# The down projection of a convolutional feed-forward layer as seven products of halves

## The chip, the cores and the metric

The kernel runs on one core of a Trainium2 chip, in one launch. The metric is the device time of that launch in microseconds (us). The engines are named as in the profile: PE does matrix products (PEld are its weight loads), DVE is the vector engine, ACT the scalar engine, POOL is GpSimd, and SP issues most transfers.

## The reference, cut to what matters

Two transformer blocks run one after the other over 512 tokens of width 1024, in float32. The change touches the last layer of the first block:

```
FFN_DIM = 2816; FFN_CONV_K = 3
def conv_ffn(hn, w_up, conv_w, conv_b, w_down):
    u = causal_dwconv(hn @ w_up, conv_w) + conv_b     # (512, 5632)
    gate, val = jnp.split(u, 2, axis=-1)
    return (jax.nn.silu(gate) * val) @ w_down         # (512, 2816) @ (2816, 1024)
h = h + conv_ffn(rms_norm(h, norm_ffn), ffn_up, ffn_conv_w, ffn_conv_b, ffn_down)
```

The second block ends in a layer of the same kind without convolution: `square(relu(h @ w_ff1)) @ w_ff2`.

## The kernel before, in words

**Products.** Every float32 operand x is split into a high part h and a low part l (`wsplit` L163, `split` L177): ACT copies x into the rounded type (h), DVE subtracts h from x (l). A product of two tiles is then three matrix instructions, h·h, h·l and l·h (`mm3` L187). So one step of contraction of 128 over 512 columns costs three matmuls of 128x512.

**Up projection.** `gemm_f` (L196) takes one weight piece of 1024x128 at a time, splits it, and makes a tile of 128 channels x 512 tokens in one PSUM bank with 24 matmuls; then it hands the bank to an `evac` function. In `ffn_conv` (L502) that function is the convolution: ACT writes `u` from the bank (L511), DVE adds the two delayed taps (L513, twice). A gate tile then gets its SiLU on ACT; a value tile is multiplied by its gate tile (L530) and split into `ah`, `al`. Tiles come as two gates, then two values.

**Down projection.** The 22 channel tiles are worked in groups of 8, 8 and 6. After each group `gemm_w` (L252) adds that group's share to `h`: for each half of the output's columns it loads weight pieces of 256x512 and runs over four token tiles. 22 tiles x 2 halves x 4 token tiles x 3 are 528 matmuls. Each finished bank is added to `h` by DVE (`add_to` L1642), in the last group by the residual step `Residual.ev` (L417), which on ACT and POOL also gathers the sums for the next norm. `ev` calls `step` when a row tile is complete, and that starts the scaled copy of the row (`row`, L454) and its transposes (`turn`, L474) for the next stage.

**The seven products.** The last layer, `ffn_relu2` (L577), already has another form of the down projection, `gemm_s` (L279), with the helper `Halves` (L539). Tokens, contraction and columns are each cut in two, and seven products of halves take the place of eight. Their left operands are sums and differences of quarters of the activations (names A11, S3, A12, A22, S1, S2, S4; `Halves.put` builds them tile by tile: one subtraction for a tile of the first half of the contraction, three additions for one of the second half). Their right operands are quarters of the weights and differences of those (`less`, L301). A product runs into a pair of PSUM banks; some products run on top of an earlier one in the same pair, after that has been added to `h`. All second-half tiles are needed from the second product on, only A11 and S3 need none of them.

**What sets the order.** The instructions are written out by Python in program order; then a scheduler with its own cost model reorders them for each engine, and each engine runs its list strictly in turn. A buffer is reused when its last reader is done: split weights have three buffers in this stage (two of pool `w`, one of `w_ffn`), raw weights `wr` four, raw weights `ws` four.

Of the kernel before, what the change touches and what calls it, by code (L numbers as in the profile page):

```python
# [16 lines left out]
T = 512  # L17
# [54 lines left out]
class Lines:  # L72


    def __init__(self, p):
        self.p = p
# [12 lines left out]
class Core:  # L89
# [106 lines left out]
    def gemm_f(self, src, nk, n, xh, xl, evac, halves=None, pieces=(), wide=False):  # L196

        tok, pieces = xh.shape[2], list(pieces)
        step = 1024 // nk // 128 * 128
        tiles = []
        for c0 in range(0, n, step):
            wh, wl = pieces.pop(0) if pieces else self.wpiece(src[:, c0:min(c0 + step, n)], pool=wide and halves is not None)
            for c in range(0, wh.shape[2], 128):
                tiles.append(((c0 + c) // 128, wh[:, :, c:c + 128], wl[:, :, c:c + 128]))
            if halves is not None:
                if len(tiles) < 2:  # L210
                    continue
                pss = [self.gbank()[:, 0:tok] for _ in tiles]
                halves()
                halves = None
                for s in range(2):
                    ts = slice(s * tok // 2, (s + 1) * tok // 2)
                    for ps, (m, wh, wl) in zip(pss, tiles):
                        for k in range(nk):
                            self.mm3(ps[:wh.shape[2], ts], wh[:, k], wl[:, k], xh[:, k, ts], xl[:, k, ts], k == 0, k == nk - 1)
                for ps, (m, wh, wl) in zip(pss, tiles):  # L220
# [183 lines left out]
class Residual:  # L404
# [24 lines left out]
    def ev_s(self, t, c0, ps, last):  # L429
        if last:  # L430
            self.ev(t, c0, 512, ps)
        else:
            add_to(self.core, self.h)(t, c0, 512, ps)

    def step(self, t):

# [65 lines left out]
def ffn_conv(core, pool, h, xh, xl, up, conv_w, conv_b, down, mid, res):  # L502
# [4 lines left out]

    def conv(s, i, ps):
        w, o = taps[s]
        u = pool.tile([128, T], F32, name=f"u{s}", bufs=4)  # L510
        nc.scalar.activation(u, ps, AF.Identity, scale=w[:, o[2] + i:o[2] + i + 1], bias=w[:, o[3] + i:o[3] + i + 1])  # L511
        for d in (1, 2):
            nc.vector.scalar_tensor_tensor(u[:, d:], ps[:, 0:T - d], w[:, o[2 - d] + i:o[2 - d] + i + 1], u[:, d:], op0=ALU.mult, op1=ALU.add)  # L513
        return u

    for f0 in range(0, nf, 8):
        n = min(8, nf - f0)
        ah = pool.tile([128, 8, T], F32R, name="ah", bufs=2)
        al = pool.tile([128, 8, T], F32R, name="al", bufs=2)
        for p0 in range(f0, f0 + n, 2):  # L520
            gate = {}

            def ev_gate(m, ps):
                u = conv(0, p0 + m, ps)
                nc.scalar.activation(u, u, AF.Silu)
                gate[m] = u

            def ev_val(m, ps):
                u = conv(1, p0 + m, ps)
                nc.vector.tensor_tensor(u, u, gate[m], op=ALU.mult)  # L530
                core.split(ah[:, p0 + m - f0], al[:, p0 + m - f0], u)

            yield from core.gemm_f(up[:, p0 * 128:p0 * 128 + 256], 8, 256, xh, xl, ev_gate, mid if p0 == 0 else None, wide=True)
            yield from core.gemm_f(up[:, F + p0 * 128:F + p0 * 128 + 256], 8, 256, xh, xl, ev_val, wide=True)

        yield from core.gemm_w(down[f0 * 128:(f0 + n) * 128], n, D, ah[:, 0:n], al[:, 0:n], *((add_to(core, h),) if f0 + n < nf else (res.ev, 2)))


class Halves:  # L539


    def __init__(self, core, pool):
        self.core, self.pool = core, pool

    def open(self, n):

        self.n = n // 2
        a, b = ([self.pool.tile([128, m, 4, 256], F32R, name=f"a{x}{m}") for x in "hl"] for m in (2, 5))
        self.parts = a, b
        self.ops = {nm: [x[:, i, 0:self.n] for x in p] for p, nms in ((a, ("A11", "S3")), (b, ("A12", "A22", "S1", "S2", "S4")))  # L550
                    for i, nm in enumerate(nms)}
# [2 lines left out]
    def room(self, m):  # L554

        if m < self.n:
            self.raw[m] = self.pool.tile([128, 3, 256], F32, name="r3", bufs=4)
            return self.raw[m][:, 0::2]
        self.raw[m] = self.pool.tile([128, 5, 256], F32, name="r5", bufs=2)
        return self.raw[m][:, 0:2]  # L560
# [16 lines left out]
def ffn_relu2(core, pool, h, xh, xl, up, down, mid, res):  # L577
    nc = core.nc
    nf = down.shape[0] // 128
    a = Halves(core, pool)  # L580
    for f0 in range(0, nf, 8):
        a.open(8)

# [7 lines left out]
        yield from core.gemm_s(down[f0 * 128:(f0 + 8) * 128], a.ops, res.ev_s if f0 + 8 == nf else lambda t, c0, ps, last: add_to(core, h)(t, c0, 512, ps))  # L591

# [1052 lines left out]
    return ev  # L1645


BUCKETS = 32
SKEW = 639

# [126 lines left out]
def first_rest(core, I):  # L1777
# [30 lines left out]
                drain(cross_attention(core, p, xh, xl, I["ca_wq"], core.kv, I["ca_wo"], res))  # L1808
    core.n_at = core.ctx.enter_context(ExitStack())
    d_h = core.tc.dram_tile([T, D], F32, name="d_h")  # L1810
    core.res = Residual(core, core.n_at.enter_context(core.pool("n_at")), h, I["norm_final"], I["g_attn_2"], d_h)
    core.d_h = d_h.rearrange("(t p) d -> p t d", p=128)

    def mid():
# [118 lines left out]
```

## Time and profile before

| what | us |
|---|---|
| median of 3 runs | 1988.88 |
| lowest and highest run | 1988.84, 1993.32 |
| the profiled execution, whole | 1998.17 |
| its span, first to last instruction | 1996.4 |
| the layer that is changed, from its first matmul to the last of the down projection | about 837 to 1208 of the span |
| the layer that already uses seven products | about 1612 to 1988 of the span |

All times in the rows below are counted from the start of that span. A row of a group of instructions gives their count, their busy time, the mean of one, and the idle time of the engine just before them with what ended it. Matmuls overlap, so a matmul of "0.39 us" does not take that long in a row of matmuls: the distance between two starts does.

### The profile page before, as it was taken

To read this page: it belongs to the slowest core of one execution; us is meant where nothing else is said; L and a number is where in the kernel's file an instruction comes from. 1 tells how busy PE (TensorE), PEld (TensorE's weight loads), DVE (VectorE), ACT (ScalarE), POOL (GpSimd) and SP (SyncE) were. 2 spreads that over 40 slices of the span, in tenths; PEclk is the share of its full clock that TensorE was granted. 3 is DMA by queue.
4 is the path that set the end of the run, shared out by engine and by line. 5 is a ranking of instruction groups with operands and counts; after the bars stand their busy time and mean duration, and the time that the engine had idled before them with its cause. 6 is when DMAs were issued, how large, how long until landed. Compare 5 with 4: busy or idle time off the path is not lost.

```text
span 1996.4 us, 27818 instructions
## 1 busy us (share of the span) xinstructions
PE 1937.1 (97%) x10748; PEld 1625.0 (81%) x10748; DVE 1227.7 (61%) x1979; ACT 884.3 (44%) x1498; POOL 322.3 (16%) x367
## 2 busy tenths in 40 slices
PE   6999999999899999999999998999999999999998
PEld 5777888888778988888888887888888888888886
DVE  3457453318966645465464556666789756876867
ACT  4533223335634444343242346557766433443434
POOL 1333223343330100200000003002243111000000
PEclk9999999999999999999999998999999999999999
DMA  6223222342365641332333335543222533315231
GB/s 172 75 69 82 75 77 90 111 149 61 101 194 193 191 137 43 108 95 94 97 95 95 95 95 164 151 123 99 62 62 82 185 121 115 112 57 159 82 98 43
DMA packets 280728, 215.02 MB, mean 108 GB/s; under 512 B 28206, under 2 KB 239812, under 8 KB 280468
## 3 DMA queue, kind: packets, MB, share of 16 engines
q1 hardware_dynamic: 261364, 205.23, 34.0%
q10 hardware_dynamic: 19232, 8.02, 1.7%
q8 instruction: 85, 1.39, 0.3%
q14 instruction: 47, 0.39, 0.1%
HBM read 195.35 MB, written 20.48 MB: 108 GB/s over the span
## 4 chain that ended last, share of the span: by engine, by line
PE 88%; DVE 6%; ACT 3%; issue 2%; POOL 1%; SPq 0%; DMA 0%; ACTq 0%; DVEq 0%; POOLq 0%
PE g L190 49%; PE s L190 27%; PE s L725 1%; PE s L739 1%; PE s L378 1%; PE p L1008 1%; DVE sbr L809 1%; PE s L713 1%; PE s L712 1%; DVE ptl L181 1%; PE o L1138 0%; PE s L1144 0%; SPq L1718 0%; PE s L1393 0%; DVE sba L810 0%
## 5 line engine op out<-in xcount | busy, mean ns | idle before, releaser
L173 ACT ACTIVATE wh<-wr 128x1024 fp32r<-128x1024 f32 x291 | 305.8, 1055 | 470.4 <-PE g L190 202.4
L190 PE MATMUL g<-xh,wh 128*128 128x512 f32 (+1 forms) x1168 | 454.7, 391 | 6.1 <-DVE rkr L899 2.4
L190 PE MATMUL g<-xl,wh 128*128 128x512 f32 (+1 forms) x1168 | 452.0, 387 | 1.8 <-DVE xl L181 1.8
L190 PE MATMUL g<-xh,wl 128*128 128x512 f32 (+1 forms) x1168 | 451.1, 387 | 0.0
L174 DVE TENSOR_TENSOR wl<-wr,wh 128x1024 fp32r<-128x1024 f32 (+1 forms) x224 | 274.9, 1230 | 280.7 <-ACT wh L173 276.2
L190 PEld LDWEIGHTS g<-xh,wh 128*128 128x128 f32 x1168 | 225.2, 193 | 50.8 <-issue 3.7
L190 PEld LDWEIGHTS g<-xl,wh 128*128 128x128 f32 x1168 | 225.4, 193 | 43.9 <-DVE xl L181 3.0
L190 PEld LDWEIGHTS g<-xh,wl 128*128 128x128 f32 x1168 | 224.8, 193 | 42.8 <-DVE wl L174 1.0
L174 POOL TENSOR_TENSOR wl<-wr,wh 128x1024 fp32r<-128x1024 f32 x67 | 169.3, 2530 | 425.1 <-ACT wh L173 412.0
L190 PE MATMUL s<-wl,ah 128*128 128x512 f32 x324 | 127.2, 393 | 0.0
L190 PE MATMUL s<-wh,al 128*128 128x512 f32 x324 | 126.5, 393 | 0.0
L190 PE MATMUL s<-wh,ah 128*128 128x512 f32 x324 | 123.9, 393 | 0.8 <-DVE h L420 0.8
L190 PE MATMUL s<-xl,wh 128*128 128x512 f32 x288 | 112.8, 392 | 0.0
L190 PE MATMUL s<-xh,wl 128*128 128x512 f32 x288 | 112.8, 392 | 0.0
L190 PE MATMUL s<-xh,wh 128*128 128x512 f32 x288 | 112.8, 392 | 0.0
L353 POOL TENSOR_TENSOR ss<-rss 128x1 f32<-128x1 f32 (+1 forms) x20 | 7.2, 362 | 448.2 <-ACT rsq L345 448.2
L173 ACT ACTIVATE wh<-ws 128x1024 fp32r<-128x1024 f32 x40 | 42.4, 1061 | 76.2 <-PE s L190 44.3
L1239 POOL TENSOR_SCALAR sy<-sy,rsm,ngate 128x128 f32<-128x128 f32 (+1 forms) x64 | 42.4, 664 | 198.8 <-DVE rsm L1237 182.8
L181 DVE TENSOR_TENSOR ptl<-s,pth 128x256 fp32r<-128x256 f32 (+3 forms) x144 | 66.7, 475 | 12.2 <-ACT pth L180 11.2
L190 PEld LDWEIGHTS s<-wh,ah 128*128 128x128 f32 x324 | 60.8, 188 | 15.1 <-issue 1.2
L190 PEld LDWEIGHTS s<-wl,ah 128*128 128x128 f32 x324 | 60.8, 188 | 14.1
L190 PEld LDWEIGHTS s<-wh,al 128*128 128x128 f32 x324 | 60.8, 188 | 13.9
(503 smaller groups left out, 3843.1 us busy)
## 6 DMA issues: line engine op xcount, KB each, us to landing
wr<-in_w_comb_dram SPq DMA_DIRECT2D x62, 512.0 KB
wr<-in_w_ff_dram SPq DMA_DIRECT2D x48, 512.0 KB
wr<-in_ffn_up_dram SPq DMA_DIRECT2D x44, 512.0 KB
wr<-in_w_in_dram SPq DMA_DIRECT2D x36, 512.0 KB
wr<-in_ffn_down_dram SPq DMA_DIRECT2D x22, 512.0 KB
wr<-in_ca_wkv_dram SPq DMA_DIRECT2D x16, 512.0 KB
ws<-in_w_ff_dram SPq DMA_DIRECT2D x16, 512.0 KB
d_gate<-ff SPq DMA_DIRECT2D x24, 256.0 KB
```

Source lines behind the costliest of these rows:

```text
L173: self.nc.scalar.activation(h, raw, AF.Copy)
L174: (self.nc.gpsimd if pool or self.lpool else self.nc.vector).tensor_tensor(l, raw, h.bitcast(F32), op=ALU.subtract)
L181: nc.vector.tensor_tensor(l, src, h.bitcast(F32), op=ALU.subtract)
L190: self.nc.tensor.matmul(out, l, r, start=start, stop=stop, skip_group_check=more)
L378: nc.tensor.transpose(ps[:, j * 128:(j + 1) * 128], x[:, j * 128:(j + 1) * 128], self.ident)
L712: mm(s, q[:, qs], kk[0][:, 0:n], start=True, stop=False)
L713: mm(s, q[:, qs], kk[1][:, 0:n], start=False, stop=last)
L725: core.nc.tensor.transpose(ps[:, c], p[:, c], core.ident)
L739: mm(o[:, c], v[:, k], x[:, k, c], start=False, stop=False)
L809: nc.vector.tensor_tensor_scan(r[:, 0:n][:, ::-1], f[:, ::-1], core.zeros(n), 1.0, op0=ALU.mult, op1=ALU.add)
L1008: mm(ps[:, j], KB[hp, j, c].rearrange("p a t -> p (a t)"), KR[hp, j, c].rearrange("p a t -> p (a t)"), start=True, stop=True)
L1239: nc.gpsimd.tensor_scalar(y, y, scalar1=rs, scalar2=fac, op0=ALU.mult, op1=ALU.mult)
```

## The change

`ffn_conv` takes `gemm_s` for its down projection in all its groups. The 22 tiles are grouped 4, 6, 6 and 6, since a group needs an even number; each operand of `gemm_s` is then 2 or 3 tiles deep. Gate and value tiles alternate: `gemm_f` is given a list of 128-column pieces, gate 0, value 0, gate 1, and so on. The buffers of `u0` and `u1` go from four to two, `Halves` gets a size (4 or 3), the raw weights pool `ws` is opened before this layer, and the residual step after it keeps its rows there.

```
@@ gemm_f
-        for c0 in range(0, n, step):
-            wh, wl = pieces.pop(0) if pieces else self.wpiece(src[:, c0:min(c0 + step, n)], pool=wide and halves is not None)
+        for i, s in enumerate(src if isinstance(src, list) else [src[:, c:min(c + step, n)] for c in range(0, n, step)]):
+            wh, wl = pieces.pop(0) if pieces else self.wpiece(s, pool=wide and halves is not None)
@@ ffn_conv
-        u = pool.tile([128, T], F32, name=f"u{s}", bufs=4)
+        u = pool.tile([128, T], F32, name=f"u{s}", bufs=2)
...
-    for f0 in range(0, nf, 8):
-        n = min(8, nf - f0)
-        ah = pool.tile([128, 8, T], F32R, name="ah", bufs=2)
-        al = pool.tile([128, 8, T], F32R, name="al", bufs=2)
...
-            def ev_val(m, ps):
-                u = conv(1, p0 + m, ps)
-                nc.vector.tensor_tensor(u, u, gate[m], op=ALU.mult)
-                core.split(ah[:, p0 + m - f0], al[:, p0 + m - f0], u)
...
-        yield from core.gemm_w(down[f0 * 128:(f0 + n) * 128], n, D, ah[:, 0:n], al[:, 0:n], *((add_to(core, h),) if f0 + n < nf else (res.ev, 2)))
+    a, gate = Halves(core, pool, 3), {}
+    f0 = 0
+    while f0 < nf:
+        n = (nf - f0) % 6 or 6
+        a.open(n)
+        def ev(i, ps):
+            m = i // 2
+            u = conv(i % 2, f0 + m, ps)
+            if i % 2 == 0:
                 nc.scalar.activation(u, u, AF.Silu)
                 gate[m] = u
+            else:
+                nc.vector.tensor_tensor(a.room(m), *(x.rearrange("p (u t) -> p u t", u=2) for x in (u, gate.pop(m))), op=ALU.mult)
+                a.put(m)
+        cols = [up[:, s * F + f * 128:s * F + (f + 1) * 128] for f in range(f0, f0 + n) for s in range(2)]
+        yield from core.gemm_f(cols, 8, n * 256, xh, xl, ev, mid if f0 == 0 else None, wide=True)
+        yield from core.gemm_s(down[f0 * 128:(f0 + n) * 128], a.ops, add_s(core, h) if f0 + n < nf else res.ev_s)
+        f0 += n
@@ first_rest
-    core.res = Residual(core, core.n_at.enter_context(core.pool("n_at")), h, I["norm_final"], I["g_attn_2"], d_h)
+    core.ws = core.n_at.enter_context(core.pool("ws"))
+    core.res = Residual(core, core.n_at.enter_context(core.pool("n_at")), h, I["norm_final"], I["g_attn_2"], d_h, core.ws)
```

The lists of the engines stay as they were outside this layer and the first projection behind it. Three places matter for what follows.

DVE, before, end of the last group: from the last value tile (its bank is `g_9732`, `u1_9757` its convolution) to the first sums that are added to `h`.

```order
L174 TENSOR_TENSOR wl_9831<-wr_9828,wh_9830 128x1024
L513 SCALAR_TENSOR_TENSOR u1_9757<-g_9732,fp1_7537,u1_9757 128x511
L513 SCALAR_TENSOR_TENSOR u1_9757<-g_9732,fp1_7537,u1_9757 128x510
L530 TENSOR_TENSOR u1_9757<-u1_9757,u0_9683 128x512
L181 TENSOR_TENSOR al_9319<-u1_9757,ah_9318 128x512
L174 TENSOR_TENSOR wl_9881<-wr_9878,wh_9880 128x1024
```

DVE, after, end of the second group (six tiles), the second part of the same stretch: `u1_8532` is the last value tile, `r5_8536` the room in which its five operand planes are built (L572 to L574), `ah5_8079` and `al5_8080` the high and low operands, `wl_...` split weights, `ws_...` raw weights that are subtracted from each other (L304).

```order
L531 TENSOR_TENSOR r5_8536<-u1_8532,u0_8496 128x512
L174 TENSOR_TENSOR wl_8628<-ws_8547,wh_8627 128x512
L304 TENSOR_TENSOR ws_8545<-wr_8587,ws_8545 128x1024
L572 TENSOR_TENSOR r5_8536<-r3_8304,r5_8536 128x256
L304 TENSOR_TENSOR ws_8547<-wr_8589,ws_8547 128x512
L304 TENSOR_TENSOR ws_8549<-ws_8549,ws_8545 128x1024
L573 TENSOR_TENSOR r5_8536<-r5_8536,r3_8304 128x256
L304 TENSOR_TENSOR ws_8551<-ws_8551,ws_8547 128x512
L174 TENSOR_TENSOR wl_8658<-ws_8547,wh_8657 128x512
L574 TENSOR_TENSOR r5_8536<-r5_8536 128x256
L181 TENSOR_TENSOR al5_8080<-r5_8536,ah5_8079 128x5x256
L1645 TENSOR_TENSOR h_5269<-g_8591,h_5269 128x512
```

Before, the last tile's operand was ready four DVE instructions after its bank; now weight work stands between its steps, and its operand comes at the end of them.

PE, before, the same end of the last group: the last three matmuls of the up projection and the first of the down projection.

```order
L190 MATMUL g_9732<-xh_7420,wh_9728 128x512
L190 MATMUL g_9732<-xl_7421,wh_9728 128x512
L190 MATMUL g_9732<-xh_7420,wl_9729 128x512
L190 MATMUL g_9764<-wh_9770,ah_9318 128x512
L190 MATMUL g_9764<-wl_9771,ah_9318 128x512
L190 MATMUL g_9764<-wh_9770,al_9319 128x512
```

PE, after, second group: the 42nd matmul of the down projection and those behind it. `g_8591` and `g_8592` are the banks of the product A12, `s_8621` and `s_8622` those of S1; `wh_8597` and `wh_8627` are the weights of the third, last tile of each.

```order
L190 MATMUL s_8622<-wh_8623,al5_8080 128x512
L190 MATMUL g_8591<-wh_8597,ah5_8079 128x512
L190 MATMUL g_8591<-wl_8598,ah5_8079 128x512
L190 MATMUL g_8592<-wh_8597,ah5_8079 128x512
L190 MATMUL g_8592<-wl_8598,ah5_8079 128x512
L190 MATMUL s_8621<-wh_8627,ah5_8079 128x512
L190 MATMUL s_8621<-wl_8628,ah5_8079 128x512
```

Where the down projection began with weights times tiles that had long been there, it now has 42 matmuls that need no plane of the last tile, and the 43rd needs one.

## Rows read from the trace of the kernel before

**Rows 1.** The page, part 1: the span; busy us, share and instructions.
```profile
span 1996.4 us, 27818 instructions
...
PE 1937.1 (97%) x10748; PEld 1625.0 (81%) x10748; DVE 1227.7 (61%) x1979; ACT 884.3 (44%) x1498; POOL 322.3 (16%) x367
```
**Rows 2.** Stretches: length, busy us of PE, PEld, DVE, ACT, POOL, granted clock, DMA.
```profile
926.00:970.00 44.00, 44.00 (x193) 35.75 (x192) 17.97 (x20) 10.78 (x12) 0.00 (x0) 1.00 0.32 95
...
1690.00:1732.00 42.00, 42.00 (x184) 34.30 (x183) 39.57 (x47) 19.42 (x19) 0.00 (x0) 1.00 0.29 88
```
**Rows 3.** Groups by form, 838 to 1212 us, the changed layer.
```profile
L174 DVE TENSOR_TENSOR wl<-wr,wh 128x1024 fp32r<-128x1024 f32 x66 | 81.7, 1239 | 141.6 <-ACT wh L173 141.6
L173 ACT ACTIVATE wh<-wr 128x1024 fp32r<-128x1024 f32 x66 | 69.8, 1060 | 109.6 <-PE s L190 74.6 <-PE g L190 30.1 <-issue 4.8
...
L190 PE MATMUL s<-wl,ah 128*128 128x512 f32 x132 | 51.9, 393 | 0.0
...
L190 PE MATMUL g<-wl,ah 128*128 128x512 f32 x44 | 17.3, 393 | 0.0
...
L511 ACT ACTIVATE u<-s,fp 128x512 f32<-128x512 f32 x21 | 16.0, 762 | 0.0
L513 DVE SCALAR_TENSOR_TENSOR u<-s,fp,u 128x510 f32<-128x510 f32 x21 | 15.7, 749 | 0.7
...
L530 DVE TENSOR_TENSOR u<-u,u 128x512 f32<-128x512 f32 x22 | 15.2, 692 | 0.8
...
L423 POOL TENSOR_TENSOR h<-h,gb 128x512 f32<-128x512 f32 x7 | 9.4, 1349 | 357.3 <-ACT rsq L345 357.3
```
**Rows 4.** The chain that ended last, 780 to 1260 us: start, us, what.
```profile
950.77 24.98 PE s L190 x108
```
**Rows 5.** Groups by form, 1690 to 1996 us, the layer with seven products.
```profile
L1644 DVE TENSOR_TENSOR h<-s,h 128x512 f32<-128x512 f32 x42 | 28.2, 684 | 20.0 <-PE s L190 20.0
L181 DVE TENSOR_TENSOR al<-r,ah 128x1280 fp32r<-128x1280 f32 x16 | 23.8, 1487 | 0.3
L180 ACT ACTIVATE ah<-r 128x1280 fp32r<-128x1280 f32 x16 | 20.2, 1265 | 10.7 <-DVE r L573 10.7
...
L303 DVE TENSOR_TENSOR ws<-wr,ws 128x1024 f32<-128x1024 f32 x15 | 18.2, 1216 | 0.0
...
L571 DVE TENSOR_TENSOR r<-r,r 128x256 f32<-128x256 f32 x15 | 6.2, 417 | 0.0
```
**Rows 6.** PE in order of time, 1698 to 1717 us: start, us, instruction.
```profile
1699.08 0.40 PE L190 MATMUL g<-xh,wl 128*128 128x512 f32 x1
...
1715.86 0.39 PE L190 MATMUL g<-wh,ah 128*128 128x512 f32 x1
```
**Rows 7.** ACT in order of time, the same stretch.
```profile
1713.16 1.25 ACT L180 ACTIVATE ah<-r 128x1280 fp32r<-128x1280 f32 x1
```
**Rows 8.** DVE in order of time, the same stretch: two neighbours.
```profile
1706.91 1.22 DVE L174 TENSOR_TENSOR wl<-ws,wh 128x1024 fp32r<-128x1024 f32 x1
1708.05 1.21 DVE L303 TENSOR_TENSOR ws<-wr,ws 128x1024 f32<-128x1024 f32 x1
```
**Rows 9.** What PE waited for, 1943 to 1985, then 838 to 1255 us: total, times, longest.
```profile
PE s L190 <- DVE h L420: 0.8, 1, 0.8
...
PE s L378 <- DVE xnt L463: 5.9, 2, 4.9
```
**Rows 10.** Stretches as in rows 2, at the layer's start.
```profile
836.00:839.60 3.60, 1.28 (x9) 0.71 (x7) 3.48 (x6) 1.89 (x5) 1.35 (x4) 0.97 0.52 154
839.60:842.00 2.40, 2.40 (x11) 2.40 (x12) 1.88 (x3) 0.00 (x0) 0.00 (x0) 0.50 0.08 21
842.00:846.00 4.00, 4.00 (x33) 4.00 (x33) 0.12 (x1) 0.00 (x0) 0.00 (x0) 0.90 0.00 0
```
**Rows 11.** PE in order of time at that start: neighbours at either clock.
```profile
842.10 0.41 PE L190 MATMUL g<-xh,wh 128*128 128x256 f32 x1
842.31 0.41 PE L190 MATMUL g<-xl,wh 128*128 128x256 f32 x1
...
844.05 0.28 PE L190 MATMUL g<-xh,wh 128*128 128x256 f32 x1
844.17 0.28 PE L190 MATMUL g<-xl,wh 128*128 128x256 f32 x1
```

More of the change, by code (lines that the diff above doesn't have):

```diff
@@ L204, in gemm_f @@
         tiles = []
-        for c0 in range(0, n, step):
-            wh, wl = pieces.pop(0) if pieces else self.wpiece(src[:, c0:min(c0 + step, n)], pool=wide and halves is not None)
+        for i, s in enumerate(src if isinstance(src, list) else [src[:, c:min(c + step, n)] for c in range(0, n, step)]):
+            wh, wl = pieces.pop(0) if pieces else self.wpiece(s, pool=wide and halves is not None)
             for c in range(0, wh.shape[2], 128):
-                tiles.append(((c0 + c) // 128, wh[:, :, c:c + 128], wl[:, :, c:c + 128]))
+                tiles.append(((i * step + c) // 128, wh[:, :, c:c + 128], wl[:, :, c:c + 128]))
             if halves is not None:
@@ L432, in ev_s @@
         else:
-            add_to(self.core, self.h)(t, c0, 512, ps)
+            add_s(self.core, self.h)(t, c0, ps, last)
     def step(self, t):
@@ L514, in conv, with __init__ @@
         return u
-    for f0 in range(0, nf, 8):
-        n = min(8, nf - f0)
-        ah = pool.tile([128, 8, T], F32R, name="ah", bufs=2)
-        al = pool.tile([128, 8, T], F32R, name="al", bufs=2)
[L520 to L524, printed above, removed]
+    a, gate = Halves(core, pool, 3), {}
[7 more added lines that the diff above has]
+            if i % 2 == 0:
                 nc.scalar.activation(u, u, AF.Silu)
                 gate[m] = u
-            def ev_val(m, ps):
-                u = conv(1, p0 + m, ps)
-                nc.vector.tensor_tensor(u, u, gate[m], op=ALU.mult)
-                core.split(ah[:, p0 + m - f0], al[:, p0 + m - f0], u)
-            yield from core.gemm_f(up[:, p0 * 128:p0 * 128 + 256], 8, 256, xh, xl, ev_gate, mid if p0 == 0 else None, wide=True)
-            yield from core.gemm_f(up[:, F + p0 * 128:F + p0 * 128 + 256], 8, 256, xh, xl, ev_val, wide=True)
-        yield from core.gemm_w(down[f0 * 128:(f0 + n) * 128], n, D, ah[:, 0:n], al[:, 0:n], *((add_to(core, h),) if f0 + n < nf else (res.ev, 2)))
+            else:
[5 more added lines that the diff above has]
+        f0 += n
 class Halves:
-    def __init__(self, core, pool):
-        self.core, self.pool = core, pool
+    def __init__(self, core, pool, size):
+        self.core, self.pool, self.size = core, pool, size
     def open(self, n):
         self.n = n // 2
-        a, b = ([self.pool.tile([128, m, 4, 256], F32R, name=f"a{x}{m}") for x in "hl"] for m in (2, 5))
+        a, b = ([self.pool.tile([128, m, self.size, 256], F32R, name=f"a{x}{m}") for x in "hl"] for m in (2, 5))
         self.parts = a, b
@@ L556, in room @@
         if m < self.n:
-            self.raw[m] = self.pool.tile([128, 3, 256], F32, name="r3", bufs=4)
+            self.raw[m] = self.pool.tile([128, 3, 256], F32, name="r3", bufs=self.size)
             return self.raw[m][:, 0::2]
@@ L579, in ffn_relu2 @@
     nf = down.shape[0] // 128
-    a = Halves(core, pool)
+    a = Halves(core, pool, 4)
     for f0 in range(0, nf, 8):
@@ L590, in ffn_relu2 @@
         yield from core.gemm_f(up[:, f0 * 128:(f0 + 8) * 128], 8, 1024, xh, xl, ev_up, mid if f0 == 0 else None, wide=True)
-        yield from core.gemm_s(down[f0 * 128:(f0 + 8) * 128], a.ops, res.ev_s if f0 + 8 == nf else lambda t, c0, ps, last: add_to(core, h)(t, c0, 512, ps))
+        yield from core.gemm_s(down[f0 * 128:(f0 + 8) * 128], a.ops, add_s(core, h) if f0 + 8 < nf else res.ev_s)
 CA_H = 4
@@ L1645, in add_to, with add_s @@
     return ev
+def add_s(core, h):
+    return lambda t, c0, ps, last: add_to(core, h)(t, c0, 512, ps)
 BUCKETS = 32
```

## The prediction

> **What bounds the kernel now.** I read the page's busy times first: PE works 97% of the span, DVE 61% [rows 1]. Then the stretches: in the up projection of the changed layer PE has no gap and DVE is at 18 of 44 us, while in the layer that already uses seven products DVE is at 39.6 of 42 us, with PE still gapless [rows 2]. So what is worth asking is not how much PE work goes, but whether DVE can still feed PE at the seam between the two projections. For that I read, in order: the groups by form, for the price of each operation [rows 3, 5]; the chain that ended last, for PE's pace [rows 4]; and the order of time at one seam of the last layer, for how long the last tile's operand takes [rows 6 to 8]. The chain through the changed layer is one run of PE pieces, so every matmul that goes is time, and so is every wait that comes.
>
> **The change part by part.**
>
> *Matmuls removed.* Before, 132 x 3 + 44 x 3 = 528 matmuls of the down projection [rows 3]. After, 22 tiles x 7 products x 3 = 462; PE's list is 66 shorter. The pace is 24.98 us for 108, 0.231 us each [rows 4]. **Minus 15.2 us.** The up projection has the same matmuls in another order: nothing.
>
> *DVE and ACT work added.* A weight quarter is split once per product instead of once: for a group of six, seven splits of 128x1024 and seven of 128x512, four subtractions of each size, 14 additions into h instead of 8, and for each second-half tile a plane of 1280 instead of 512. Of these the 128x512 weight split and subtraction aren't in the trace; the nearest rows are the product of 128x512 on DVE, 0.69, and on ACT a 512-wide pass between half the 1024 split's 1.06 and the 0.76 of the convolution [rows 3]. I take 0.69 and 0.63, since the first is the same operation and size; below zero is excluded, they are additional work. In the down projection of six tiles DVE's sum is 7 x (1.22 + 0.69) + 4 x (1.22 + 0.69) + 14 x 0.68 = 30.5 us, of which about 0.08 per hand-over overlaps (a split of 1.22 is followed after 1.14 [rows 8]): 27.5. PE has 126 x 0.231 = 29.1. With the 1280-wide last tile on top, DVE is full there, so order decides.
>
> *The seam, where the change adds its wait.* Take the second group and count from the end of the up projection's last matmul. PE then has 42 matmuls that don't need the last tile (18 of A11, 12 of A12, 12 of S1): 42 x 0.231 = 9.7 us. The 43rd needs the high half of the last tile's planes. Its way there: ACT first splits the first weights of A12, whose buffer that very tile has just freed (1.06), DVE the low half (1.14); by then ACT has also written the convolution's first term (0.76) and DVE is at 2.2 us. Up to the last of the three additions DVE's list then holds 17 instructions: two taps (2 x 0.75), two additions into h (2 x 0.69), the previous tile's 1280-wide split (1.49), a 128x1024 weight split (1.22) and three of 128x512 (3 x 0.69), the product (0.69), three plane additions (3 x 0.42), two subtractions of 1024 (2 x 1.22) and two of 512 (2 x 0.69): 13.4 us by [rows 3, 5], less 17 x 0.085 for the hand-overs [rows 8] = 11.9. So 14.1 us, plus 1.27 for ACT's high split [rows 5]: **15.4 us against 9.7, a wait of 5.7 us.** The nearest measured case is the last layer's own seam: its last up matmul starts at 1699.08, ends its turn 0.23 later, and the last tile's high split ends at 1714.41: 15.1 us [rows 6, 7]. There PE had 72 matmuls in hand, eight-tile groups being four deep, and came to the first dependent one at 1715.86, 1.4 us after the operand. Same length of chain, 42 matmuls instead of 72: that is the whole argument. The fourth group has the same list. In the third S2's first weights find a buffer earlier and 54 matmuls stand in front, but those weights are split at 14.4 us: PE loses 4.4. The first group, two deep, has 30 matmuls (6.9 us) and a chain of 12.1: 5.2. **Plus 5.2 + 5.7 + 4.4 + 5.7 = 21.0 us.**
>
> *Behind the seam.* While PE waits, weight splits queue behind the last tile on DVE, and S2's first weights get a buffer only when A12 or S1 is done with it. Second group: at 15.4 PE has 16 more matmuls (to 19.1); DVE does the low split (1.4), four additions into h (2.4) which must precede the products that run on the same banks, and the split (1.14): S2's second matmul goes at 21.3, 2.2 later; another 0.6 where A22 follows S3 in the same banks. The same walk gives 2.8 for the first and fourth group (five or six additions stand before S4's weights), 4.1 for the third. **Plus 12.5 us**; bounds 0.8 per group, the one such wait that the last layer shows [rows 9], and 5.
>
> The Trainium skill bears on this ("Perfetto Trace Analysis", section "Matmuls" under "Optimizing Tensor Performance"): independent matmul groups should rotate through banks, so that evacuation overlaps the next group; running S2 to A22 on just-read banks goes against it. The 0.8 us above says that this is harmless when DVE is on time; by the page each of the four late products would wait for an addition, and the sum would be some 3 us higher.
>
> *The clock.* At the layer's start PE was busy for 1.28 of 3.6 us, and the granted clock then stood at 0.50, the lower of the two levels (1.2 GHz), and came back within the next stretch [rows 10]; matmuls started 0.21 us apart instead of 0.12 for about 14 of them [rows 11], 1.3 us lost. A wait of over 5 us should cost the same. **Plus 4 x 1.3 = 5.2 us**, bounds 0 and 6.
>
> *The tail.* In the last group rows 0 and 1 are complete after S4, 36 matmuls before the end, rows 2 and 3 together at the end, where before one row followed the other. The gap at that place is 5.9 us of PE waiting for the scaled rows [rows 9]. POOL's passes of 1.35 over h [rows 3], two per row, and the row sums set it; they start from S4 on and are as many as before, so the last row is done some 9 to 14 us after the last matmul either way, and half of the next stage's first tiles can run in between. I take 0, bounds -4 and +4.
>
> *Without a price.* Weights: the same bytes, in smaller pieces; SP's list puts the next group's up pieces behind the down pieces, and they wait for S4's weights to be split (about 22 us after the seam) but are needed at 33 or later; the transfer engines are at a third [rows 2]. Two buffers of u instead of four: each is read two tiles (11 us) before its next use. If a transfer took over 10 us, it would cost the difference once a group.
>
> Sum: -15.2 + 21.0 + 12.5 + 5.2 + 0 = **+23.5 us**. The profiled execution took 1998.2 with a span of 1996.4 [rows 1], 9 us above the median of the runs, 1988.9; on the profile this gives 2021.7, on the median 2012.
>
> **The rivals.**
>
> *The cover is enough (faster).* If the last tile's chain is under some 10 us, PE never waits and the 15.2 us stay: 1974. For it: the last layer shows exactly this at eight tiles [rows 6, 7], and the scheduler put 42 matmuls in front because its own costs said so. Against it: the measured durations; the chain would have to shrink by a third. It decides at 9.7 us from the last up matmul to the end of the last high split.
> The skill gives the same outcome by a rule ("Perfetto Trace Analysis", section "Identifying the Most-Contended Engine"): improve the engine with the highest occupancy first, and that is PE here. The whole span's 97% agrees; the 39.6 of 42 us on DVE at a seam doesn't.
>
> *Waits, but half (about the same).* If the second waits fall to the 0.8 per group of the last layer and the first ones to 4 because fillers are pushed behind the chain: -15.2 + 16 + 3.2 = +4, 1993; without the clock's share this is the floor of my case.
>
> *The waits pile up (slower still).* If the slow clock delays the additions into h and so the next weights, every group loses 5 us behind the seam, and the tail 4: -15.2 + 21 + 20 + 5.2 + 4 = +35, 2024.
>
> **How the numbers follow.** My case has 0.70 (2000 to 2020), the pile-up 0.06, half waits 0.11, enough cover 0.13. A measurement of this kernel can tell about 0.3%, 6 us, from no change, that is 1983 to 1995. Faster: 0.13. The same: all of half waits, 0.11. Slower: 0.76. The range takes in my case, most of half waits and the pile-up's centre: 1990 to 2024; the case of enough cover is left out.
>
> **What would show it.** In the changed profile, in the window of each down projection: PE waiting on ACT ah (L180) for 4 to 6 us at the first product behind A11 and S1, then on DVE wl (L174) or h (L1645) for 2 to 4; DVE over 90% busy in those stretches; a granted clock of 0.5 to 0.8 just after each wait; 66 matmuls fewer. Wrong would be: no wait on ah, or the tile's chain under 10 us; a wait on a transfer; or a gap at the next projection that differs from 5.9 us by more than 4.

## The result and the profile after

| | before | after |
|---|---|---|
| median on the same chip, us (4 runs each) | 1991.1 | 2023.54 |
| ratio, 95% interval | | 1.014 (1.0121 to 1.0159) |
| the profiled execution, us | 1998.17 | 2024.36 |
| its span, us | 1996.4 | 2022.6 |

The changed kernel is slower by 32 us on the medians, by 28 by the ratio, and by 26 us on the two spans. The median of 1991.1 rests on four runs, two of them at 1988.8; on three other chips the same kernel's medians were 1995.3 to 1996.4, of 13 to 19 runs each, so of these numbers the lower ones are probably nearer the truth. The spans differ from the rest at the front: nothing changed ahead of this layer, but its first matmul stands at 836.85 us of the span before and at 832.75 after. Counted from that matmul to the end of the span, the change costs 1189.9 - 1159.6 = **30.3 us**, and this is the sum that the rest of the text divides.

The page of the changed kernel, part 1, answers [rows 1]:

```profile
span 2022.6 us, 27861 instructions
...
PE 1936.7 (96%) x10682; PEld 1615.3 (80%) x10682; DVE 1313.1 (65%) x2110; ACT 906.7 (45%) x1525; POOL 321.9 (16%) x367
```

PE has 10682 matmuls instead of 10748, the 66 fewer that were counted. Its busy time has hardly fallen (1937.1 before), because matmuls at the lower clock are longer in it. DVE has 85 us more.

What PE waited for in the changed layer and at the next projection, 838 to 1245 us, answers the second half of [rows 9] (us in total, times, longest):

```profile
PE g L190 <- ACT ah L180: 10.8, 3, 5.0
PE s L190 <- DVE wl L174: 6.9, 9, 2.0
PE s L379 <- DVE ws L464: 4.9, 2, 3.8
PE s L190 <- DVE h L1645: 3.2, 4, 0.9
PE s L190 <- ACT wh L173: 3.2, 6, 1.2
PE g L190 <- DVE u L514: 2.0, 1, 2.0
```

Before, that layer had no wait of PE after its start. Now there are 26 us of them at the four seams, and the longest kind is the forecast one: the high half of the last tile's planes. The chain that ended last, at the second seam (start, us, what), shows the whole list between PE's last up matmul, at 979.94, and the operand, at 995.51:

```profile
979.94 1.07 ACT wh L173
...
981.03 1.23 DVE wl L174
982.26 0.66 DVE u L514
982.92 0.60 DVE h L1645
983.51 1.40 DVE al L181
984.91 0.66 DVE u L514
985.58 0.60 DVE h L1645
986.17 1.73 DVE wl L174 x2
987.91 0.60 DVE r L531
988.51 0.60 DVE wl L174
989.11 1.14 DVE ws L304
990.25 0.34 DVE r L572
990.58 1.74 DVE ws L304 x2
992.32 0.33 DVE r L573
992.65 0.60 DVE ws L304
993.26 0.60 DVE wl L174
993.86 0.35 DVE r L574
...
994.23 1.28 ACT ah L180
```

DVE has no gap in it. Only six of its pieces are the last tile's own: two taps (L514), the product (L531) and three additions (L572 to L574) take 2.9 us together; weights (L174, L304), the tile before (L181) and additions into h (L1645) take the rest.

The four seams as stretches, with the columns of [rows 2]:

```profile
883.65:918.63 34.98, 29.11 (x107) 21.19 (x106) 24.26 (x30) 9.68 (x10) 0.00 (x0) 0.90 0.28 83
979.94:1020.99 41.05, 33.39 (x130) 25.15 (x129) 29.48 (x38) 14.86 (x17) 0.00 (x0) 0.92 0.34 103
1086.40:1127.19 40.79, 35.13 (x130) 26.00 (x129) 29.27 (x38) 14.86 (x17) 0.00 (x0) 0.92 0.35 103
1192.57:1232.20 39.63, 32.32 (x127) 24.04 (x125) 30.79 (x38) 18.60 (x30) 8.97 (x9) 0.96 0.20 57
```

Before, such a stretch was gapless at a granted clock of 1.00 [rows 2]. For a sum I use one measure throughout: from the first matmul of a group's down projection to its last, less 0.2315 us for each matmul in between. By it the kernel before loses 0.0, 0.0 and 0.1 us in its three groups, and the changed kernel **10.7, 11.2, 11.0 and 10.5, together 43.3 us**. With 66 x 0.2315 = 15.3 us of matmuls gone that is +28.0 of the 30.3; the stretch behind the last down matmul is 1.4 us longer, and the layer's start takes the last 0.9.

### The profile page after: what moved, and what is told of

Read it like the earlier page. It is cut to its first block, busy times and chain, and to the rows that moved or that the text cites. A ratio compares the mean times of both kernels' runs of the same rounds, so it can differ in the third digit from the quotient of the medians.

```text
span 2022.6 us, 27861 instructions
## 1 busy us (share of the span) xinstructions
PE 1936.7 (96%) x10682; PEld 1615.3 (80%) x10682; DVE 1313.1 (65%) x2110; ACT 906.7 (45%) x1525; POOL 321.9 (16%) x367
## 4 chain that ended last, share of the span: by engine, by line
PE 83%; DVE 9%; ACT 3%; issue 2%; POOL 1%; DMA 1%; SPq 1%; ACTq 0%; DVEq 0%; POOLq 0%
PE g L190 47%; PE s L190 26%; DVE wl L174 1%; PE s L726 1%; PE s L740 1%; DVE h L1645 1%; PE s L379 1%; PE p L1009 1%; ACT wh L173 1%; DVE sbr L810 1%; PE s L714 1%; PE s L713 1%; DVE ptl L181 1%; DVE ws L304 1%; PE o L1139 0%
## 5 line engine op out<-in xcount | busy, mean ns | idle before, releaser
L173 ACT ACTIVATE wh<-wr 128x1024 fp32r<-128x1024 f32 (+2 forms) x283 | 294.0, 1045 | 442.6 <-PE g L190 207.0
L174 DVE TENSOR_TENSOR wl<-wr,wh 128x1024 fp32r<-128x1024 f32 (+2 forms) x216 | 261.6, 1216 | 194.1 <-ACT wh L173 189.5
L174 POOL TENSOR_TENSOR wl<-wr,wh 128x1024 fp32r<-128x1024 f32 x67 | 169.2, 2529 | 423.1 <-ACT wh L173 410.0
L173 ACT ACTIVATE wh<-ws 128x1024 fp32r<-128x1024 f32 (+1 forms) x75 | 73.0, 974 | 132.8 <-PE s L190 70.5
L174 DVE TENSOR_TENSOR wl<-ws,wh 128x1024 fp32r<-128x1024 f32 (+1 forms) x75 | 83.4, 1115 | 27.8 <-ACT wh L173 27.6
L180 ACT ACTIVATE ah<-r 128x512 fp32r<-128x512 f32 (+1 forms) x54 | 51.2, 948 | 77.4 <-DVE r L568 55.4
L190 PEld LDWEIGHTS s<-wl,ah 128*128 128x128 f32 x324 | 62.6, 193 | 24.7 <-DVE wl L174 10.5
L1645 DVE TENSOR_TENSOR h<-s,h 128x512 f32<-128x512 f32 x84 | 56.1, 685 | 36.7 <-PE s L190 36.7
```

Of the source, the lines that this page charges most:

```text
L173: self.nc.scalar.activation(h, raw, AF.Copy)
L174: (self.nc.gpsimd if pool or self.lpool else self.nc.vector).tensor_tensor(l, raw, h.bitcast(F32), op=ALU.subtract)
L180: nc.scalar.activation(h, src, AF.Copy)
L190: self.nc.tensor.matmul(out, l, r, start=start, stop=stop, skip_group_check=more)
L1645: core.nc.vector.tensor_tensor(h[:, t, c0:c0 + w], ps, h[:, t, c0:c0 + w], op=ALU.add)
```

## The experiments

Times are differences of the medians to the kernel before on the same chip; "one run" marks what was timed once. Executions differ by some us ahead of this layer, so the loss at the seams, in the last columns, is the firmer number.

| kernel | time to before, us | loss at each seam, us | sum |
|---|---|---|---|
| the change | +32.4 | 10.7, 11.2, 11.0, 10.5 | 43.3 |
| alternation alone | +0.5 | 0.0, 0.0, 0.1 | 0.0 |
| no weight differences | +5.5, one run | 9.2, 4.5, 2.1, 4.1 | 19.9 |
| four buffers | +11.5, one run | 6.7, 3.6, 3.4, 4.2 | 17.9 |
| both of these | +2.6, one run | 5.6, 0.5, 0.3, 1.2 | 7.5 |
| groups 8, 8, 6 | +22.0 | 6.2, 6.2, 14.9 | 27.4 |
| groups 4, 4, 4, 4, 6 | +43.5, one run | 10.5, 10.8, 11.3, 11.4, 13.9 | 57.8 |
| differences on POOL | +29.8 | 11.6, 11.5, 7.6, 11.7 | 42.4 |
| gate tiles behind A11 | +5.5 | 0.0, 3.1, 2.4, 10.9 | 16.4 |
| the same, four buffers | -5.1 | 0.5, 0.6, 0.3, 4.2 | 5.5 |
| the same, another start | -3.1 | 0.4, 0.6, 0.3, 5.8 | 7.1 |
| before, last layer with three buffers | +24.2 | 5.7, 5.6, 4.1, 11.6 (last layer) | 27.1 |

**Alternation alone.** The kernel before with the new order of tiles, the old down projection and its groups of 8, 8 and 6.

```
-        for p0 in range(f0, f0 + n, 2):
-            ... two gates, then two values ...
+        cols = [up[:, s * F + f * 128:s * F + (f + 1) * 128] for f in range(f0, f0 + n) for s in range(2)]
+        yield from core.gemm_f(cols, 8, n * 256, xh, xl, ev, mid if f0 == 0 else None, wide=True)
```

> The alternation of gate and value tiles alone; groups of 8, 8, 6 and the old down projection stay, with all 528 matmuls. My theory puts the whole loss at the seams in front of the seven products, so this should be the kernel before within 3 us: no wait of PE in the up projection, and the last tile's operand still only four DVE instructions behind its bank. The rival that the order of the tiles costs by itself (a value tile's longer vector work in every pair) would give 10 us or more over before.

1995.76 against 1995.26, ratio 0.9996 (0.9982 to 1.0011). The alternation is free, and so are the two buffers of `u0` and `u1` instead of four, which this kernel keeps from the change; everything lies in the down projection.

**No weight differences.** `less` does nothing in this layer, so S2, S4, S3 and A22 run on plain quarters of the weights. This leaves out a part of the computation.

```
             for d, x, y in zip(own[dst], own[a], own[b]):
-                nc.vector.tensor_tensor(d, x, y, op=ALU.subtract)
+                if self.ld:
+                    nc.vector.tensor_tensor(d, x, y, op=ALU.subtract)
```

> The changed kernel without the differences of weight quarters (the subtraction on DVE is left out, so the products use plain quarters; every matmul, split and addition stays). Theory of the chain: two subtractions of 1024 and two of 512 stood between the last tile's steps on DVE, 3.5 us of its 15.6; so in the six-tile groups the wait on ah falls from 5.0 to about 1.5 us and the whole kernel loses some 12 to 18 us less, ending 8 to 16 us over before. Rival, the three buffers of split weights set the pace: the wait on ah falls, but S2's weights still come only when a buffer is free, and the kernel stays 20 us or more over before.

+5.5 us, less than the 8 to 16 expected. Of the chain above, two subtractions of 1.14 and two of 0.60 us go, 3.5 us. What PE waited for in this layer, 850 to 1245 us:

```profile
PE g L190 <- ACT ah L180: 4.1, 4, 2.2
PE s L190 <- DVE h L1648: 2.4, 3, 0.9
PE s L190 <- DVE wl L174: 2.3, 4, 0.6
```

Four subtractions a seam take more than half of the loss away, so DVE's work at the seam is a cause. Whether by its total (1291 instead of 1313 us, 22 less, where the seams lose 23 less) or by its place in the list, this run can't tell; the kernel with woven gates and four buffers does, below.

**Four buffers.** The change with four instead of three buffers of split weights (and one instead of two of `u1`, to make room).

```
-        u = pool.tile([128, T], F32, name=f"u{s}", bufs=2)
+        u = pool.tile([128, T], F32, name=f"u{s}", bufs=2 - s)
...
-    with core.weights(1, "w_ffn", 0), core.pool("ffn") as p:
+    with core.weights(2, "w_ffn", 0), core.pool("ffn") as p:
```

> The changed kernel with four buffers of split weights instead of three (u of the value tiles has one buffer instead of two, to make room). Theory of the chain: the wait on ah stays near 5 us in the six-tile groups, since it is DVE's list and not a buffer that delays the operand; only the waits on wh and wl behind it shrink, together 10.1 us in all groups, so the kernel ends 14 to 22 us over before. Rival of the buffers: the waits in front and behind go, 25 us or more are won, and the kernel ends at or below before.

+11.5, more than a buffer was thought to give: the wait on `ah`, expected to stay near 5 us, is 2.4 at the longest. The chain at the second seam, whose first down matmul starts at 981.43:

```profile
981.59 4.20 PE s L190 x18
...
991.44 1.06 ACT wh L173
992.49 1.17 ACT ah L180
...
993.71 1.19 PE g L190 x4
```

The chain no longer begins with a weight split that waits for the last tile's buffer. The 42 matmuls run without a break, and the operand is there 12.2 us after the first down matmul instead of 15.6; of what remains, 1.06 us is one weight split that ACT takes first. The waits on `wl` and `wh` are gone from the list of waits. I had not asked for the price of a buffer in the prediction, only for the list.

**Both remedies.** Four buffers and no weight differences, which leaves out the same part of the computation.

> The changed kernel with both single remedies: four buffers, and the four weight differences of each group left out (so that S2, S4, S3 and A22 run on plain quarters of the weights, which is another result). Alone they gave +11.5 and +5.5 us beside the kernel before, where the change itself has about +30. If the two causes are separate they add up to -11 to -15 us (the matmuls' gain of 15.2 is the floor). If they are one cause seen twice (DVE's list in front of the last tile), the second adds little: 0 to +5 us.

+2.6 in one run, outside the -11 to -15 that separate causes would have given and inside the 0 to +5 of one cause seen twice, yet the seams say something else: they lose 7.5 us, 5.6 of it at the first, and the three six-tile groups 0.5, 0.3 and 1.2. So at the seams the two together remove nearly everything; the rest of the time is elsewhere. The layer's start has a wait of 4.6 us for xl instead of 2.0, as in all kernels with four buffers that keep the start's splits (below), and the gap behind the last down matmul has waits of 6.3 us on the scaled rows; from that matmul to the end of the span this execution takes 6.6 us longer than the kernel before. A sum of times from single spans would have hidden that.

**Deeper groups.** Groups of 8, 8 and 6 with three buffers; 72 matmuls then stand in front of the last tile's operand in two of the groups. Room came from single buffers of `r5`, `u1` and of the rows of the norm ahead.

```
-    a, gate = Halves(core, pool, 3), {}
+    a, gate = Halves(core, pool, 4, 1), {}
...
-        n = (nf - f0) % 6 or 6
+        n = min(8, nf - f0)
```

> The seven products in groups of 8, 8 and 6 tiles instead of 4, 6, 6, 6: operands up to four tiles deep, room made by fewer buffers elsewhere (one for the five planes, one of u for value tiles, one row buffer in the norm before). Theory of the chain: PE has 66 to 78 matmuls (15 to 18 us) in hand at the seams of the two large groups, as in the last layer, so no wait on ah there; the third group loses its 11 us as now. Against before: -15.2 + 11 + 2 to 6 for small waits, so within -3 to +4 us. Rival, DVE is full whatever the depth: 10 us or more lost at each of the three seams, 15 us or more over before.

1.0091 (1.0068 to 1.0113), +22 us on the medians and +18 by the ratio, where -3 to +4 was expected: my theory of depth failed here. By the seams alone it would be -15.3 + 27.4 = +12; the rest lies outside them: in the profiled execution 5.6 us behind the last down matmul, and part at the layer's start, where PE now waits for xnt twice, 2.0 us at the longest, probably for the single buffer of rows. What causes the 5.6 us stays open. But both deep groups still lose 6.2 us, and the last layer loses nothing with groups of the same depth. That left one difference that I had overlooked: that layer has four buffers of split weights, this one three.

**The last layer with three buffers.** One number in the kernel before.

```
-    with core.weights(2, "w_mlp"), core.pool("mlp") as p:
+    with core.weights(1, "w_mlp"), core.pool("mlp") as p:
```

> The kernel before, with one number changed: the last layer, which has had seven products all along, gets three buffers of split weights instead of four. Theory A (three buffers are too few for the seven products, because the last tile of the up projection holds one of them and each product needs two): this layer, gapless so far, gets waits at its four seams, on ACT wh L173 and DVE wl L174 and on the operand ah L180, of 3 to 6 us a seam: +12 to +25 us. Theory B (depth decides: with eight tiles 72 matmuls stand in front of the last tile's operand, and that is what hides the chain): no more than 1 us a seam, -1 to +4 us, as the list in front of that operand is not what the number changes. Between these: the buffer is one cause beside others.

1.0116 (1.009 to 1.0142), +24 us, the upper end of theory A; theory B is out. What PE waited for in that layer, 1690 to 2016 us, where [rows 9] has 0.8 us:

```profile
PE g L190 <- DVE al L181: 4.1, 3, 1.4
PE s L190 <- ACT wh L173: 3.4, 5, 1.2
PE s L190 <- DVE h L420: 2.6, 1, 2.6
...
PE s L190 <- DVE wl L174: 1.8, 4, 0.6
PE g L190 <- ACT ah L180: 1.2, 4, 0.4
```

And its chain at the first seam, which before was matmuls from end to end:

```profile
1699.20 4.18 PE s L190 x18
...
1703.40 1.07 ACT wh L173
...
1704.49 1.23 DVE wl L174
```

Behind these the chain is DVE without a gap to 1721.6. The layer that was my measured case was gapless because of its depth *and* its fourth buffer: with three, each product's second weights wait until PE has finished with the product before, their splits come late and in a row, and the last tile's steps queue among them. The Trainium skill points there ("Perfetto Trace Analysis", section "Optimization Strategy"): a gap that repeats regularly on the engine that should be full can mean too little memory for the next tile to be allocated, its buffer count among the reasons. These 24 us agree.

**Five seams.** The same matmuls and the same weights split, one seam more.

```
-        n = (nf - f0) % 6 or 6
+        n = 4 if f0 < nf - 6 else 6
```

> The changed kernel with the 22 tiles grouped 4, 4, 4, 4 and 6: five seams instead of four, the same matmuls, the same weights split, the same additions into h. If the loss belongs to the seam (a chain of fixed length behind the last tile against 30 or 42 matmuls in hand), it grows by one seam, 10.5 us: about +38 to +43 us beside the kernel before. If it is DVE's total work that is too much, the sum stays: +27 to +33 us.

+43.5 us in one run; the seams lose 57.8 instead of 43.3. A seam of four tiles, with a third less of weights to split than one of six, loses as much as that, 10.5 to 11.4 us, so the loss looks like one of the seam. This run doesn't decide it, though, since the expectation has one thing wrong: the additions into h aren't the same. A group makes 14 of them whatever its size, 70 in all instead of 56, and DVE is busy for 1323 us instead of 1313. That total work alone is not the cause is shown by the kernel with woven gates and four buffers, below. That the one of six tiles now loses 13.9 instead of 10.5 us was not expected, and its cause stays open.

**The differences on POOL.**

```
-                nc.vector.tensor_tensor(d, x, y, op=ALU.subtract)
+                (nc.gpsimd if self.lp else nc.vector).tensor_tensor(d, x, y, op=ALU.subtract)
```

> The changed kernel with its three buffers, and the weight differences (L304) on POOL instead of DVE. If DVE's list in front of the last tile's operand is half of the cause, as the kernel without these differences showed (+5.5), this gives about the same, +5 to +12 us. If passes of DVE are stretched while POOL works on large tiles (at this layer's start a row pass on DVE took 3.36 instead of 1.28 us beside a split of 2.35 us on POOL), the chain loses again what it gained: +15 to +30 us.

1.0158 (1.0135 to 1.0181), +30 us: as slow as the change. The chain at the second seam has no subtraction any more, but its DVE passes have become longer:

```profile
983.42 0.35 DVE r L575
...
983.79 2.49 DVE r L576
...
987.61 3.48 DVE al L181
```

POOL at the same time (start, us, engine, line, operation):

```profile
982.57 4.84 POOL L304 TENSOR_TENSOR ws<-wr,ws 128x1024 f32<-128x1024 f32 x2 [7.41 <-DVE wl L174]
```

In the changed kernel the same addition of 128x256 takes 0.35 in the chain and the split 1.40. What the chain gained, the stretched passes took back, as the second case of the expectation had it.

**Gate tiles behind A11.** The next group's first two gate tiles, 48 matmuls that need nothing of this seam, are worked between A11 and A12, their weights' low halves on POOL; three buffers.

```
+        early = [(0, 0), (1, 0)] if f0 + n < nf else []
+        raws = [core.wraw(c) for c in cols(f0 + n, early)]
+        seven = core.gemm_s(down[f0 * 128:(f0 + n) * 128], a.ops, add_s(core, h) if f0 + n < nf else res.ev_s)
+        next(seven)
+        yield
+        f0 += n
+        if early:
+            yield from tiles(f0, early, None, [core.wsplit(r, True) for r in raws])
+        yield from seven
```

> The changed kernel, still with three buffers, but the next group's first two gate tiles (48 matmuls, 11.1 us) are worked between A11 and A12, with their weights' low halves on POOL. If the last tile's chain against the matmuls in hand is the cause (15.6 us against 9.7), these 48 matmuls cover it: no wait on ACT ah L180 over 1 us, and the time is -15.2 plus what is left behind the seam, 2 to 4 us in each of three groups, plus 11 us in the last group, which has no next one: 0 to +6 us beside the kernel before. If DVE as a whole is the limit in the down projection (30 us of work against 29 us of matmuls), the 48 matmuls bring DVE only two convolution terms each (1.5 us) and 11 us of room, which gives the same sign; the two part in the waits behind: throughput leaves none, order and buffers leave wl and h. If three buffers are the limit, the wait stays, now on ACT wh L173 or DVE wl L174: +10 to +20 us.

1.0023 (1.0009 to 1.0036), +5.5 us, at the upper end of the first case. The three seams with a next group lose 0.0, 3.1 and 2.4 us, with no wait on `ah` left, only two or three of about 1 us on `wl` and h. The fourth, which has no next group, still loses 10.9, with the wait of 5.0 us on `ah`.

**The same with four buffers.**

> The same with four buffers of split weights. Cover and buffers together: in three of four seams no wait over 1 us, in the last one 4 us as in the kernel with four buffers alone, and perhaps the 5 us at the layer's start that that kernel showed: -15.2 + 4 + 3 + 0 to 5 = -8 to -3 us beside the kernel before. If the waits are due to neither, it stays above +5 us.

0.9973 (0.9963 to 0.9983), -5.1 us, as expected. It is a small gain, 0.3%, though the interval is clear of no change; beside the change as it was given it is some 33 us by the two ratios, 37 by the medians. Its seams, as stretches (columns of [rows 2]):

```profile
887.40:925.58 38.18, 38.18 (x164) 30.50 (x163) 31.98 (x40) 16.42 (x19) 0.00 (x0) 1.00 0.34 101
973.76:1014.91 41.15, 41.15 (x176) 32.69 (x175) 35.38 (x44) 17.78 (x22) 2.40 (x1) 1.00 0.36 111
...
1165.75:1198.87 33.12, 29.78 (x127) 23.15 (x125) 28.96 (x37) 16.78 (x32) 8.41 (x11) 1.00 0.23 64
```

In the first three (the third, left out here, reads as the second) PE is busy throughout at a granted clock of 1.00, while DVE is at 84 to 86% of the stretch; only the last has gaps. DVE's total is that of the change, 1315 us for 1313, though in this kernel POOL makes the low halves of the six early weight pieces. So over the layer DVE can do this work in time, and it was the order and the buffers, not the total, that cost nearly all of the 43 us. The Trainium skill ("Perfetto Trace Analysis", section "Optimization Strategy") also says this: where the most-contended engine changes from one part of a kernel to the next, weaving these parts together can help. These runs agree: weaving took the loss from 43.3 to 16.4 us with three buffers and from 17.9 to 5.5 with four.

**Another start.** The same, with the layer's second weight piece split on DVE instead of POOL.

```
-            wh, wl = pieces.pop(0) if pieces else self.wpiece(s, pool=wide and halves is not None)
+            wh, wl = pieces.pop(0) if pieces else self.wpiece(s, pool=wide and halves is not None and not (tiles and isinstance(src, list)))
```

> The kernel with the two gate tiles behind A11 and four buffers, and the layer's second weight piece split on DVE instead of POOL, so that nothing large runs on POOL beside the row pass that precedes the first matmuls. If POOL's split stretches that pass (3.36 against 1.28 us) and so makes the wait of 4.6 us for xl L187 at the layer's start, the wait falls to 2 to 3.5 us, since DVE has the split of 1.2 us instead: -5 to -8 us beside the kernel before. If not, the wait stays or grows, and so does the time: -5 to -3 us.

0.9986 (0.9974 to 0.9998), -3.1 us, not to be told from -5.1, and short of the -5 to -8 expected if the stretched pass makes the wait. Locally it did part of what it should: the row pass on DVE is 1.28 instead of 3.36 us, and the wait for xl fell from 4.6 to 3.6, not to 3.5 or less. The split on DVE took the rest of that gain, and the last seam lost 1.6 us more in this execution.

## Why the prediction was right, and where it was not

The forecast of slower held, and 2023.5 us lies in the range, but only by half a microsecond: it is outside the 2000 to 2020 of the case that had 0.70, and two of the four runs lie above 2024. The mechanism, waits at the seam behind the last tile's operand, was right; that the number fell inside the range is partly luck, since two of its terms missed in opposite directions. Step by step:

*Matmuls removed, -15.2.* Right: 66 fewer, at 0.2315 us.

*The first waits, +21.0.* Right in kind at the second and fourth seam, and nearly in size. At the second seam the walk through DVE's list gave 15.4 us from the last up matmul to the operand; the chain shows 15.6, with the same instructions in the same order. The wait is 5.0 us for the forecast 5.7, at the fourth seam 5.0 as well; the first seam gives 2.0 + 1.4 + 0.7 = 4.1 for 5.2, the third 1.2 + 2.0 = 3.2 for 4.4. Together 17.3. At the first seam only 0.7 of it is on `ah`; the 2.0 are on `u` L514, that is on a bank that the last tile's taps still had to read, which the walk did not have. The trace counts a wait from the modelled end of a matmul, so a wait is longer in PE's pace than it is told: between the matmuls at 1202.80 and 1208.18 lie 5.38 us, of which 4.99 are told as wait and 0.23 are the pace, which leaves 0.16.

*Behind the seam, +12.5.* Somewhat too much: 9.1 us (1.7, 2.6, 2.5 and 2.3), on `wh`, `wl` and h as forecast but for 0.4 on the row sums. The rule of the Trainium skill on rotating banks ("Perfetto Trace Analysis", section "Matmuls") is borne out in part: PE waits on h L1645 once at the first seam, once at the second and twice at the third, 3.2 us in all, near the 3 us that the sentence on it gave. It isn't due to the banks alone, though: with four buffers alone these waits are still 3.1 us, but with four buffers and either of the other remedies one of 0.8 us is left.

*The clock, +5.2.* **This is the term that was mis-sized.** The seams lose 43.3 us and the waits are 26.4; the other 16.9 us are the lower clock and the hand-overs. By the granted clock of the four stretches (0.90, 0.92, 0.92 and 0.96 over 35.0, 41.1, 40.8 and 39.6 us) the clock would take 3.5 + 3.3 + 3.3 + 1.6 = 11.7 us, but 3.7 us of the time at the lower level fell into waits, where it costs nothing. By the starts of the matmuls, 49 at the lower level, without a told wait, take 2.6 + 2.0 + 3.2 + 1.5 = 9.4 us more than 0.2315 each. Another 4.6 us is what the 24 waits cost beyond their told length, and some 3 are gaps too short to be told as waits; for these 7.6 us the sum had no term. My 1.3 a seam came from one short return of the clock at the layer's start [rows 10, 11]; here the matmuls behind the wait at 1208.18 ran at the lower level, and smaller waits followed:

```profile
1202.80 0.39 PE L190 MATMUL s<-wh,al 128*128 128x512 f32 x1
1208.18 0.79 PE L190 MATMUL g<-wh,ah 128*128 128x512 f32 x1 [4.99 <-ACT ah L180]
1208.77 0.63 PE L190 MATMUL g<-wl,ah 128*128 128x512 f32 x1
1209.20 0.63 PE L190 MATMUL g<-wh,ah 128*128 128x512 f32 x1
```

Starts 0.43 apart instead of 0.23 are the level of 1.2 GHz. At the first and third seam the clock fell too (0.90 and 0.92 above), though no single wait there is told as longer than 2.0 us; the forecast had it fall behind waits of over 5. Waits forecast 7 us too large and a rest 12 us too small partly cancelled: 38.7 forecast, 43.3 measured.

*The tail, 0.* Right: 1.4 us. The waits for the scaled rows at the next projection are 4.9 us, 5.9 before [rows 9].

*"Same length of chain, 42 matmuls instead of 72: that is the whole argument."* **This step failed**, though the time did not depend on it. Seventy-two matmuls in hand are not enough: with three buffers they lose 6.2 us a group here and 4.1 to 11.6 in the last layer itself. And 42 are nearly enough with four buffers (3.4 to 4.2 us). The walk had both effects in it, since it let A12's first weights wait for the last tile's buffer, but I named depth as the cause, and never asked how many buffers the measured case had.

*DVE over 90% busy.* Half right: 13.16 of 15.6 us from the second seam to its operand, 13.41 of 14.5 at the third, 84 and 92%. The gaps in it are ACT's 1.07 us at the start and 1.33 at the high split's end.

*The base.* The forecast on the profiled execution was 2021.7 and that came out at 2024.4. Taking 9 us off for the median was the larger error: the changed kernel's runs lie between 2019.1 and 2025.7 us, and its profiled one is no outlier among them. Nor was the profiled 1998.2 of the kernel before: on three other chips its medians were 1995.3 to 1996.4, so the 1988.9 was probably the low one.

*The rivals.* Enough cover was to be decided at a chain of 9.7 us; it is 15.6. Half waits fell with the 5.0 us on `ah`. The pile-up was meant as 5 us behind each seam, and that is 1.7 to 2.6; its total came closest only because of the clock.

## What to carry to other kernels

A form of a product that splits more operands for fewer matmuls has to be paid for at the seam where its left operands are just being finished, so walk the feeding engine's list there and compare it with the matmuls in hand, but count the buffers too: a layer next door that runs the same form without a gap is only a witness if its buffers are the same. What repairs such a seam is independent matmuls put into it (43.3 us of loss to 16.4 here) and one more buffer of split weights (to 17.9), and only both together (5.5) turned the change into a gain, of 5 us. Price waits on PE with the slower matmuls and the hand-overs that come with them, not alone: here 26.4 us of waits came with 16.9 us of those.

## What the runs showed of the hardware

A pass on DVE over two operands can take more than twice its time while POOL works on a large tile. At the start of the kernel with woven gates and four buffers, POOL's split and DVE's row pass began within 0.1 us of each other:

```profile
832.82 2.35 POOL L180 TENSOR_TENSOR wl<-wr,wh 128x1024 fp32r<-128x1024 f32 x1
```

```profile
829.57 1.28 DVE L475 SCALAR_TENSOR_TENSOR xnt<-h,rrs,gb 128x1024 f32<-128x1024 f32 x1 [0.43 <-POOL rrs L459]
...
832.89 3.36 DVE L475 SCALAR_TENSOR_TENSOR xnt<-h,rrs,gb 128x1024 f32<-128x1024 f32 x1
```

The same pass takes 1.28 us alone and 3.36 beside POOL; the 2.1 us more are nearly the rest of POOL's 2.35. The Trainium skill has this as a rule ("SBUF — State Buffer", section "SBUF: two separate sides"): DVE passes with two operands in SBUF and GpSimd share a pair of ports, and the one that comes first keeps it for its whole instruction. These rows agree. So does the other direction: POOL's pass of 128x1 over the row mean (L454), 0.19 us at 828.71, took 1.23 at 830.99, beside a weight split of 1.23 us that DVE had begun at 830.94. The kernel with the differences on POOL agrees in part: 2.49 instead of 0.35 and 3.48 instead of 1.40 us, while the addition of 0.35 us just before, which the profile puts into the same time of POOL, was not longer. Why that one was spared stays open; the profile's spans on POOL are rough.
